# A hybrid GLA / short-convolution layer in fp32r on one core: w_up by 256-column matmuls, nine raw buffers, and attention steps moved

## The chip, the cores and the metric

The kernel runs on one core of a Trainium2 chip. The metric is the device time of one execution in microseconds (us). Three executions of the kernel before took 1450.29, 1451.01 and 1453.19 us; the median is 1451.01 us. One further execution was profiled; it took 1448.84 us, and the profile's span, from the first to the last instruction, is 1447.1 us of that.

## The reference

One layer (DEPTH = 1) over 256 frames of 2048 channels, all in float32:

```python
mod = silu(c) @ w_ada + b_ada                     # 6 vectors of 2048: sh1 sc1 g1 sh2 sc2 g2
h = rmsnorm(x, g0) * (1 + sc1) + sh1
q,k,v,r,lr,cb,cc,cx,ga,gb = split(h @ w_in)       # 512 512 1024 1024 16 1024 1024 1024 2048 2048
log_a = log_sigmoid(lr @ w_a2 + b_a2) / 16
o = gla(q * 128**-.5, k, v, log_a)                # 4 heads, chunks of 64 frames, gated state
y_a = (rmsnorm(o, gla_norm_g) * silu(r)) @ w_out_gla
y_b = (cb * conv3(cc * cx)) @ w_out_conv
x = x + g1 * rmsnorm((sigmoid(ga)*y_a + sigmoid(gb)*y_b) @ w_o, g1n)
h = rmsnorm(x, g2n) * (1 + sc2) + sh2
gate, up = split(h @ w_up)                        # 2 x 5632
x = x + g2 * rmsnorm((gelu(conv3(gate)) * up) @ w_down, g3n)
```

`conv3` is a causal depthwise convolution over three frames. `gla` reads, for each frame of a chunk of 64, the state after that chunk.

## The kernel before

**Arithmetic.** Every large product is made of three TensorE products in the type fp32r. Weights and activations are each split into a high part and a rest: hi is the value cast to fp32r, lo is the value minus hi. A product is hi*hi + hi*lo + lo*hi, accumulated in PSUM.

**Weights** come in chunks of 512 KB (256 rows by 512 columns) by one DMA from SyncE's queue (L278) into a rotating buffer named `raw`. ScalarE casts `raw` to `whi` (L283), VectorE subtracts to make `wlo` (L292). Six `raw` buffers and four of each `whi` and `wlo` rotate. A chunk's `raw` buffer comes free when `wlo` has been made.

**Two forms of product.** `Feat` (L346) keeps the weights as the stationary operand and streams the activations, so its output has channels on partitions and frames in columns. `Tok` (L401) keeps the activations stationary and streams 512 weight columns. `Feat` makes 512 output channels as four blocks of 128 (index j). The activations stand in one tile `H`, for each block of 128 channels 576 columns wide: the first 256 are lo, the next 256 are hi, and behind them, for the feed-forward part, two columns for a shift. For most groups the four blocks share one PSUM tile `mm` of two banks, 256 columns each (`pair=True`). Three `mm` tiles rotate. Two single banks `sm` serve all small products.

**w_up** (`ffn`, 11 pairs of groups, gate and up) is different. The first pair (g = 0) runs on activations that are not yet normalised, by products of 258 columns. For the other 20 groups `both` is set: each block has a whole bank, one matmul of `whi` streams the 512 columns lo and hi of `H` together, and one of `wlo` streams the 256 columns hi into the second half. The two halves of the bank are summed afterwards in `added`: ScalarE copies the first half out (L974), VectorE adds the second (L975). So each chunk (2 blocks of rows, 4 of channels) takes 8 matmuls of 512 and 8 of 256 columns. Then the gate is convolved (`conv`, L616 and L618) and goes through gelu, and the up part is multiplied with it.

**Order.** The whole kernel is a list `stream` of chunks: w_ada's first two vectors together with w_in, then w_in's rest, w_out_conv, w_in's ga, w_out_gla, w_o, and the feed-forward part. Between the chunks stand rows of w_ada for the later vectors (`Gemv`, L439: VectorE multiplies one 512 KB raw buffer with one column of silu(c) and adds it to an accumulator). `pump` walks the list: it issues DMAs up to 10 chunks ahead (`LOOK_DMA`) but never more than the number of raw buffers ahead of the splitting, splits four chunks ahead, and issues the matmuls. A scheduler then sets each engine's order by its own estimate; each engine runs its list strictly in order.

**The attention in the background.** After every chunk of matmuls, `pump` takes one step of a generator `bg`. Beside w_out_conv (24 chunks with w_in's last group ahead of it) that is `gla_gates`: sigmoid of gb, the forget gate, the decayed keys. Beside ga (32 chunks) it is `gla_then_gates`: first `silus` (L670, L671: SiLU of r, four steps), then `gla_heads` with eight steps for each of four heads, then the four sigmoids of ga. That is 36 steps ahead of the sigmoids for 32 chunks; what is left is issued at once (`run_all`). A head is: k^T v (L758), state (L763), q^T S (L772), squares (L776), their sum (L779), a product with ones (L782), square root (L785), reciprocal (L786), scaling (L790, L792), split (L634, L635). The split results are w_out_gla's moving operand, so w_out_gla's last quarter of rows needs the fourth head. `to_rows("g1")` (L819 to L827) sends the vector g1 to memory and back as a row on all partitions.

**Into the feed-forward part.** w_o's last group runs one half of the frames after the other; each half's squares (L833), square root (L850, written r), reciprocal and the new x (L1138) follow, and transposes of x on TensorE (L1152).

Of the kernel before, what the change touches and what calls it, by code (L numbers as in the profile page):

```python
# [15 lines left out]
P = 128  # L16
T = 256
# [20 lines left out]
RAW_BUFS, SPLIT_BUFS, LOOK_SPLIT, LOOK_DMA = 6, 4, 4, 10  # L38
# [23 lines left out]
def hybrid_layer(ctx, tc, x, c, w_ada, b_ada, norm_g, w_in, w_a2, b_a2, gla_norm_g,  # L62
# [127 lines left out]
    def moving():  # L190

        t = sb([P, KD * H_ROW + 32], "H", 1, F32R)[:, 0:KD * H_ROW].rearrange("p (k n) -> p k n", k=KD)
        return t[:, :, T:], t[:, :, 0:T], t[:, :, 0:2 * T]

    h_hi, h_lo, _ = moving()
# [104 lines left out]
    class Feat:  # L300
# [5 lines left out]
        def __init__(self, w, n0, kts, hi, lo, post, row0=0, pair=True, cols=T, per=4, acc=None, both=None):  # L306
            self.both = both
# [17 lines left out]
        def mm(self, ch):  # L325
# [4 lines left out]
            def products(j, passes):  # L330
# [5 lines left out]
                for t in range(ch.n):  # L336
                    for i in passes:
                        w, m = ((ch.hi, self.hi), (ch.hi, self.lo), (ch.lo, self.hi))[i]
                        cols = T if i == 1 else self.cols
                        if self.both and i == 1:  # L340
                            continue
                        if self.both:
                            out, x = (dst[:, T:], m(ch.k0 + t, T)) if i else (dst, self.both(ch.k0 + t))
                        else:
                            out, x = dst[:, 0:cols], m(ch.k0 + t, cols)
                        nc.tensor.matmul(  # L346
                            out, w[:, t, j * P:(j + 1) * P], x,
                            start=first_in_bank and t == 0 and i == 0, stop=end and t == ch.n - 1 and i == 2,
                            skip_group_check=True)
# [335 lines left out]
    def gla_gates():  # L685
# [12 lines left out]
        ps = sm_bank()  # L698
        for k in range(KD):
# [46 lines left out]
    def gla_heads():  # L746
        yield from silus(sr["t"][:, 0])
# [53 lines left out]
    def post_ya(g):  # L801
        def post(j, v):
            if not m_t:
                m_t["hi"], m_t["lo"], _ = moving()
# [162 lines left out]
    xb = lambda k: xs["both"][:, k, :]  # L967
# [4 lines left out]
    def added(dst, ps):  # L972

        nc.scalar.copy(dst, ps[:, :, 0:T])  # L974
        nc.vector.tensor_add(dst, ps[:, :, T:], dst)  # L975
# [9 lines left out]
    def post_gate(g):  # L985
        def post(j, ps):
            if j == 0:
                gl[g] = sb([P, 4, T], "c4", 2)
            pt = padded()
            if g >= N_RAW:  # L990
                added(pt[:, :, 2:], ps)
            else:
                t, b = normed(ps)
                for a in range(2):
                    nc.scalar.activation(pt[:, a, 2:], t[:, a, :], AF.Identity, bias=b[:, a:a + 1])
            cv = tiles(t2())
            conv(cv, pt, lambda i, a: fw(i, 4 * g + j + a))
# [119 lines left out]
    bg = to_rows("g1", gg1, "g8", G8, og["last"])  # L1117
    pump(6, each=step_bg)
# [11 lines left out]
    with tc.high_priority():  # L1130
        xs["hi"], xs["lo"], xs["both"] = moving()
# [90 lines left out]
```

## Time and profile before

| what | value |
|---|---|
| three executions | 1450.29, 1451.01, 1453.19 us |
| the profiled execution | 1448.84 us, its span 1447.1 us |
| granted TensorE clock, mean | 0.993 |
| TensorE busy | 1407.4 us, 97% of the span |
| VectorE, ScalarE busy | 1058.6 us (73%), 816.9 us (56%) |
| read from memory | 363.18 MB, 252 GB/s over the span |
| w_in and w_ada, w_out_conv, w_out_gla, w_o | up to about 695 us |
| feed-forward part | from about 695 us to the end |

Matmuls overlap, and their ends are modelled: a matmul of 256 columns has a mean duration of 278 ns in the groups but starts much closer to the one before. So TensorE's busy share tells little of the pace; that is read from counts over a stretch of time. In a row of the waits the first name waits for the second, with total us, times, and the longest. In a timeline the bracket at the end gives the engine's idle time before the row and what ended it.

### The profile page before, as it was taken

The numbers are of one execution on the slowest core, as the hardware profiler recorded it, in microseconds if no ns is written. First come the engines' busy times: TensorE is split into PE (matmuls) and PEld (weight loads), VectorE is DVE, ScalarE is ACT, GpSimd is POOL, SyncE is SP. The second block draws the span as 40 slices with busy tenths as digits, with TensorE's granted clock in tenths as the row PEclk, the third lists the DMA queues.
The fourth block names the chain that finished last, engine by engine and source line by source line (L and its number), as shares of the span: only waits on it lengthen the run. The fifth ranks groups of instructions, "written<-read, shape, count | busy, mean of one in ns | idle before, by whom it ended". The sixth has DMA issues, their size and how long they took to land.

```text
span 1447.1 us, 23205 instructions
## 1 busy us (share of the span) xinstructions
PE 1407.4 (97%) x9107; PEld 1262.5 (87%) x9107; DVE 1058.6 (73%) x1194; ACT 816.9 (56%) x995; POOL 6.1 (0%) x40
## 2 busy tenths in 40 slices
PE   6999999999999998999999999999999999999997
PEld 6898999898999998988898888888888888888886
DVE  6878888888888777976798777556767645566565
ACT  5789776688574554444665554444545533445553
POOL 0000000000000000000000000000000000000000
PEclk9999999999999999999999999999999999999999
DMA  9999999998979777897467777777786656666652
GB/s 318 329 329 329 373 317 334 335 307 293 355 249 327 244 257 269 293 313 246 134 201 243 227 243 231 248 236 233 230 251 202 217 195 190 186 196 190 190 185 95
DMA packets 177896, 366.82 MB, mean 253 GB/s; under 512 B 13803, under 2 KB 26457, under 8 KB 177018
## 3 DMA queue, kind: packets, MB, share of 16 engines
q1 hardware_dynamic: 176857, 362.17, 76.0%
q0 software_dynamic: 352, 2.11, 0.4%
q8 instruction: 71, 1.16, 0.3%
q10 hardware_dynamic: 576, 1.05, 0.2%
q14 instruction: 40, 0.32, 0.1%
HBM read 363.18 MB, written 2.11 MB: 252 GB/s over the span
## 4 chain that ended last, share of the span: by engine, by line
PE 76%; DMA 11%; DVE 7%; ACT 3%; issue 2%; SPq 0%; DVEq 0%; ACTq 0%
PE mm L346 50%; PE mm L401 25%; DMA raw<-in_w_ada_dram 7%; DMA raw<-in_w_in_dram 4%; DVE wlo L292 2%; ACT whi L283 1%; DVE c L439 1%; DVE c L479 1%; DVE fold L211 0%; PE sm L1152 0%; ACT mm L323 0%; DVE raw L209 0%; PE sm L782 0%; ACT t L257 0%; DVE XF L1138 0%
## 5 line engine op out<-in xcount | busy, mean ns | idle before, releaser
L283 ACT CAST whi<-raw 128x1024 fp32r<-128x1024 f32 (+1 forms) x503 | 513.1, 1025 | 499.1 <-PE mm L346 202.9
L292 DVE TENSOR_TENSOR wlo<-raw,whi 128x1024 fp32r<-128x1024 f32 (+1 forms) x503 | 594.7, 1190 | 245.9 <-ACT whi L283 242.0
L346 PE MATMUL mm<-H,whi 128*128 128x256 f32 (+2 forms) x3712 | 656.9, 321 | 2.2 <-ACT H L254 1.2
L346 PEld LDWEIGHTS mm<-H,whi 128*128 128x128 f32 x3712 | 527.8, 189 | 51.5 <-ACT whi L283 1.7
L346 PE MATMUL mm<-H,wlo 128*128 128x256 f32 (+1 forms) x2496 | 365.9, 278 | 1.4 <-DVE wlo L292 1.4
L346 PEld LDWEIGHTS mm<-H,wlo 128*128 128x128 f32 x2496 | 332.6, 188 | 14.4 <-DVE wlo L292 1.6
L401 PE MATMUL mm<-whi,g 128*128 128x512 f32 x704 | 178.3, 391 | 0.0
L401 PEld LDWEIGHTS mm<-whi,g 128*128 128x128 f32 x704 | 131.9, 188 | 29.1
L439 DVE SCALAR_TENSOR_TENSOR c<-raw,sil,c 128x1024 f32<-128x1024 f32 x90 | 115.3, 1281 | 42.3 <-DMA raw<-in_w_ada_dram 42.1
L401 PE MATMUL mm<-whi,H 128*128 128x512 f32 x448 | 117.5, 394 | 4.2 <-ACT whi L283 4.2
L401 PEld LDWEIGHTS mm<-whi,H 128*128 128x128 f32 x448 | 82.9, 188 | 24.0 <-ACT whi L283 6.4
L401 PE MATMUL mm<-wlo,g 128*128 128x512 f32 x352 | 98.1, 392 | 0.0
L479 DVE SCALAR_TENSOR_TENSOR c<-raw,sil,c 128x768 f32<-128x768 f32 (+2 forms) x73 | 78.6, 1077 | 8.8 <-DMA raw<-in_w_ada_dram 8.1
L401 PEld LDWEIGHTS mm<-wlo,g 128*128 128x128 f32 x352 | 66.1, 188 | 14.1
L401 PE MATMUL mm<-wlo,H 128*128 128x512 f32 x224 | 65.3, 393 | 0.0
L439 DVE SCALAR_TENSOR_TENSOR cb<-raw,sil,cb 128x1024 f32<-128x1024 f32 x30 | 38.5, 1284 | 24.8 <-DMA raw<-in_w_ada_dram 24.8
L401 PEld LDWEIGHTS mm<-wlo,H 128*128 128x128 f32 x224 | 42.2, 188 | 9.0
L618 DVE SCALAR_TENSOR_TENSOR t<-pt,fcol,t 128x256 f32<-128x256 f32 x88 | 36.6, 481 | 0.0
L346 PE MATMUL mm<-B,whi 128*128 128x256 f32 x256 | 33.4, 283 | 0.0
L346 PEld LDWEIGHTS mm<-B,whi 128*128 128x128 f32 x256 | 30.8, 188 | 2.6 <-issue 1.2
L346 PE MATMUL mm<-g,whi 128*128 128x256 f32 x256 | 32.3, 279 | 0.0
L346 PEld LDWEIGHTS mm<-g,whi 128*128 128x128 f32 x256 | 30.8, 190 | 0.0
(196 smaller groups left out, 740.8 us busy)
## 6 DMA issues: line engine op xcount, KB each, us to landing
raw<-in_w_up_dram SPq DMA_DIRECT2D x176, 512.0 KB, 4.3
raw<-in_w_ada_dram SPq DMA_DIRECT2D x160, 512.0 KB, 5.5
raw<-in_w_in_dram SPq DMA_DIRECT2D x145, 512.0 KB, 5.5
raw<-in_w_down_dram SPq DMA_DIRECT2D x88, 512.0 KB, 4.3
raw<-in_w_o_dram SPq DMA_DIRECT2D x32, 512.0 KB, 5.5
raw<-in_w_ada_dram SPq DMA_DIRECT2D x32, 384.0 KB, 5.6
raw<-in_w_out_conv_dram SPq DMA_DIRECT2D x16, 512.0 KB, 5.3
raw<-in_w_out_gla_dram SPq DMA_DIRECT2D x16, 512.0 KB, 5.0
```

Of the source, the lines that this page charges most:

```text
L283: nc.scalar.copy(self.hi, self.raw)
L292: nc.vector.tensor_sub(self.lo, self.raw, f(self.hi))
L346: nc.tensor.matmul(out, w[:, t, j * P:(j + 1) * P], x, start=first_in_bank and t == 0 and i == 0, stop=end and t == ch.n - 1 and i == 2, s ...
L401: nc.tensor.matmul(self.out[s], m(c.k0 + t, T)[:, s * P:(s + 1) * P], w[:, t, :], start=first and t == 0 and i == 0, stop=end and t == c.n ...
L439: nc.vector.scalar_tensor_tensor(a, self.raw, sil[:, self.k:self.k + 1], a, op0=ALU.mult, op1=ALU.add)
L479: nc.vector.scalar_tensor_tensor(a, raw, sc, a, op0=ALU.mult, op1=ALU.add)
L618: nc.vector.scalar_tensor_tensor(dst[:, a, :], pt[:, a, i:T + i], w(i, a), dst[:, a, :], op0=ALU.mult, op1=ALU.add)
```

## The change

Four edits.

- `w_up`: the 20 groups that had `both` now use `pair=True`: three matmuls of 256 columns (`whi` with hi, `whi` with lo, `wlo` with hi) into the same 256 columns of PSUM, four blocks to one `mm` tile. Nothing is left to add: `added` is gone. `post_up` multiplies straight from PSUM. `conv_of` convolves the gate straight from PSUM, with the first two frames handled by shorter operands, so that the padded copy `pt` is not made for these groups. In the last chunk of a group all four blocks end together and `post` is called for two blocks at a time.
- `RAW_BUFS` goes from 6 to 9 and `LOOK_DMA` from 10 to 13. The 12 KB per partition that this takes come from `dynamic_dma_scratch_size`, now 4096 bytes.
- The four `silus` steps stand in `gla_gates`, beside w_out_conv, ahead of the small product with the low-rank gate. `gla_heads` starts with the first head.
- The sigmoids of ga stand in a new generator with `to_rows("g1")`, beside w_out_gla; ga's `done` test is gone.

```diff
-RAW_BUFS, SPLIT_BUFS, LOOK_SPLIT, LOOK_DMA = 6, 4, 4, 10
+RAW_BUFS, SPLIT_BUFS, LOOK_SPLIT, LOOK_DMA = 9, 4, 4, 13
...
-                        if self.both and i == 1:
-                            continue
-                        if self.both:
-                            out, x = (dst[:, T:], m(ch.k0 + t, T)) if i else (dst, self.both(ch.k0 + t))
-                        else:
-                            out, x = dst[:, 0:cols], m(ch.k0 + t, cols)
                         nc.tensor.matmul(
-                            out, w[:, t, j * P:(j + 1) * P], x,
+                            dst[:, 0:cols], w[:, t, j * P:(j + 1) * P], m(ch.k0 + t, cols),
...
         ps = sm_bank()
+        yield from silus(sr["t"][:, 0])
         for k in range(KD):
...
     def gla_heads():
-        yield from silus(sr["t"][:, 0])
...
-    def added(dst, ps):
-
-        nc.scalar.copy(dst, ps[:, :, 0:T])
-        nc.vector.tensor_add(dst, ps[:, :, T:], dst)
+    def conv_of(dst, v, w):
+
+        for a in range(2):
+            nc.scalar.mul(dst[:, a, :], v[:, a, :], w(2, a))
+            for i in (1, 2):
+                nc.vector.scalar_tensor_tensor(dst[:, a, i:], v[:, a, 0:T - i], w(2 - i, a), dst[:, a, i:],
+                                               op0=ALU.mult, op1=ALU.add)
...
-                added(t, ps)
-                nc.vector.tensor_mul(t, t, gl[g][:, j:j + 2, :])
+                nc.vector.tensor_mul(t, ps, gl[g][:, j:j + 2, :])
...
-                ffn += Feat(w_up[0], c0, KD, xh, xl, post, pair=False, cols=T + 2,
-                            both=xb if g >= N_RAW else None).chunks()
+                raw = g < N_RAW
+                ffn += Feat(w_up[0], c0, KD, xh, xl, post, pair=not raw, cols=T + 2 if raw else T, per=2).chunks()
...
-    def gla_then_gates():
-        yield from gla_heads()
-        yield from sigmoids(ga_t["t"], lambda g: ga_t["done"] > g)
-
-    bg = gla_then_gates()
+    bg = gla_heads()
     pump(stream.index(gla_to) + 1 - pos[2], each=step_bg)
     run_all(bg)
...
-    bg = to_rows("g1", gg1, "g8", G8, og["last"])
-    pump(6, each=step_bg)
+
+    def gates_then_row():
+        yield from sigmoids(ga_t["t"])
+        yield from to_rows("g1", gg1, "g8", G8, og["last"])
+
+    bg = gates_then_row()
+    pump(10, each=step_bg)
...
-    nc = _bacc.Bacc("TRN2", target_bir_lowering=False, num_devices=1)
+    nc = _bacc.Bacc("TRN2", target_bir_lowering=False, num_devices=1, dynamic_dma_scratch_size=4096)
```

In the changed kernel the lines behind the first edits have smaller numbers: L346 is L339, L772 is L765, L779 is L772, L782 is L775, L833 is L826, L850 is L843.

**Place 1: TensorE in a w_up group behind the first pair.** `mm` is PSUM, `H` the activations, `whi` and `wlo` the split weights of a chunk. Before:

```order
L346 MATMUL mm_8611<-H_7713,whi_8563 128x512 x4
L346 MATMUL mm_8612<-H_7713,whi_8563 128x512 x4
L346 MATMUL mm_8611<-H_7713,wlo_8565 128x256 x4
L346 MATMUL mm_8612<-H_7713,wlo_8565 128x256 x4
L346 MATMUL mm_8611<-H_7713,whi_8585 128x512 x4
```

After:

```order
L339 MATMUL mm_8313<-H_7719,whi_8239 128x256 x16
L339 MATMUL mm_8313<-H_7719,wlo_8241 128x256 x8
L339 MATMUL mm_8313<-H_7719,whi_8269 128x256 x16
L339 MATMUL mm_8313<-H_7719,wlo_8271 128x256 x8
L339 MATMUL mm_8313<-H_7719,whi_8309 128x256 x16
```

A chunk went from 8 + 8 matmuls on two `mm` tiles to 16 + 8 on one.

**Place 2: TensorE at the fourth head, where ga ends and w_out_gla begins.** `sm_6453` and `sm_6331` are the head's q^T S, `t_991` and `t_982` its sums of squares, `mm_6135` and `mm_6159` the last group of ga, `mm_6427` and `mm_6451` the first group of w_out_gla (its operand `g` is the heads' result). Before:

```order
L346 MATMUL mm_6135<-H_172,wlo_6355 128x256 x8
L772 MATMUL sm_6453<-g_110_527,c_974_6344 128x64 x8
L346 MATMUL mm_6427<-g_850_5453,whi_6390 128x256
L346 MATMUL mm_6427<-g_851_5454,whi_6390 128x256
...
L346 MATMUL mm_6427<-g_850_5453,wlo_6392 128x256
L782 MATMUL sm_6466<-t_991_6464,ones_68 128x256
L346 MATMUL mm_6427<-g_850_5453,wlo_6392 128x256 x7
```

After:

```order
L765 MATMUL sm_6331<-g_113_533,c_963_6224 128x64 x8
L339 MATMUL mm_6159<-H_172,whi_6267 128x256 x16
L339 MATMUL mm_6159<-H_172,wlo_6269 128x256 x8
L339 MATMUL mm_6159<-H_172,whi_6300 128x256 x16
L339 MATMUL mm_6159<-H_172,wlo_6302 128x256 x8
L775 MATMUL sm_6407<-t_982_6372,ones_68 128x256
L339 MATMUL mm_6159<-H_172,whi_6344 128x256 x16
L339 MATMUL mm_6159<-H_172,wlo_6346 128x256 x8
L339 MATMUL mm_6159<-H_172,whi_6376 128x256 x16
L339 MATMUL mm_6159<-H_172,wlo_6378 128x256 x8
L339 MATMUL mm_6451<-g_841_5336,whi_6411 128x256
```

The head's product with ones stood 17 matmuls behind its q^T S, inside w_out_gla's first chunk; it now stands 48 matmuls (two chunks) behind it and two chunks ahead of w_out_gla.

**Place 3: ScalarE at the end of w_o.** The rows are the squares of the second last half, its square root r, and a weight cast. Before:

```order
L283 CAST whi_7638<-raw_7550 128x1024
L833 ACTIVATE t_1198_7682,ys_179<-mm_7531 128x512
L850 ACTIVATE r_38_180<-r_38_180,eps_70 128x1
L283 CAST whi_7656<-raw_7556 128x1024
L833 ACTIVATE t_1199_7706,ys_179<-mm_7532 128x512
L850 ACTIVATE r_38_180<-r_38_180,eps_70 128x1
```

After:

```order
L283 CAST whi_7644<-raw_7507 128x1024
L826 ACTIVATE t_1201_7688,ys_179<-mm_7537 128x512
L843 ACT_TABLE_LOAD
L843 ACTIVATE r_38_180<-r_38_180,eps_70 128x1
L283 CAST whi_7662<-raw_7513 128x1024
L826 ACTIVATE t_1202_7712,ys_179<-mm_7538 128x512
```

ScalarE's last function before this place was a square root (the fourth head's); it is now a sigmoid of ga, and a load of the square root's table stands between the squares and r.

More of the change, by code (lines that the diff above doesn't have):

```diff
@@ L300, in hybrid_layer, with __init__ @@
     class Feat:
-        def __init__(self, w, n0, kts, hi, lo, post, row0=0, pair=True, cols=T, per=4, acc=None, both=None):
-            self.both = both
+        def __init__(self, w, n0, kts, hi, lo, post, row0=0, pair=True, cols=T, per=4, acc=None):
             self.w, self.n0, self.kts, self.hi, self.lo = w, n0, kts, hi, lo
@@ L803, in post @@
             if not m_t:
[L804 removed]
+                m_t["hi"], m_t["lo"] = moving()
             k = 4 * g + j
@@ L988, in post @@
                 gl[g] = sb([P, 4, T], "c4", 2)
-            pt = padded()
+            cv = tiles(t2())
+            w = lambda i, a: fw(i, 4 * g + j + a)
             if g >= N_RAW:
-                added(pt[:, :, 2:], ps)
+                conv_of(cv, ps, w)
             else:
+                pt = padded()
                 t, b = normed(ps)
```

10 lines of the change are left out of this document (4 added, 6 removed).

## The prediction

> **What bounds the kernel now.** I began with the page's busy times and the chain of waits by engine.
>
> ```profile
> PE 1407.4 (97%) x9107; PEld 1262.5 (87%) x9107; DVE 1058.6 (73%) x1194; ACT 816.9 (56%) x995; POOL 6.1 (0%) x40
> PE 76%; DMA 11%; DVE 7%; ACT 3%; issue 2%; SPq 0%; DVEq 0%; ACTq 0%
> ```
>
> TensorE sets the end for most of the span. Where it does, only its pace counts; where DMA, VectorE and ScalarE are on the chain, one must ask whether TensorE stood still. The busy time by stretches tells the two apart (columns: span, then busy us and instruction count of TensorE, its weight loads, VectorE, ScalarE, GpSimd, then clock, DMA share, GB/s):
>
> ```profile
> 150.00:170.00 20.00, 20.00 (x179) 20.00 (x178) 17.07 (x16) 15.17 (x16) 0.00 (x0) 1.00 1.04 385
> 375.00:450.00 75.00, 75.00 (x653) 71.51 (x652) 66.78 (x70) 44.80 (x50) 0.00 (x0) 1.00 0.87 302
> 450.00:575.00 125.00, 117.50 (x981) 114.17 (x980) 96.49 (x104) 62.89 (x69) 1.18 (x2) 0.97 0.80 263
> 780.00:860.00 80.00, 80.00 (x463) 69.69 (x462) 57.60 (x63) 39.00 (x47) 0.31 (x3) 1.00 0.75 238
> ```
>
> From top to bottom: w_in by 256-column matmuls, w_out_conv with the forget gate, ga with the heads, and w_up with 512 and 256 columns mixed. In w_up nothing but TensorE is near its limit. In 450 to 575 us TensorE is idle 7.5 us while the DMA engines are busy only 0.80 of the time. The waits of TensorE between 100 and 600 us name the places:
>
> ```profile
> PE sm L782 <- DVE t L779: 6.3, 2, 5.9
> PE mm L401 <- ACT whi L283: 2.2, 3, 1.0
> PE sm L1093 <- DVE gg L872: 1.9, 1, 1.9
> PE mm L346 <- DVE wlo L292: 1.4, 1, 1.4
> PE sm L782 <- DVE s L870: 1.2, 1, 1.2
> ```
>
> Together 13.0 us; this is all that the edits outside w_up can win.
>
> **The change part by part.**
>
> *w_up.* The groups by shape give the count, the chain in order of time gives the pace (start, us, what, count):
>
> ```profile
> L346 PE MATMUL mm<-H,whi 128*128 128x512 f32 x1280 | 340.2, 395 | 0.0
> 129.30 55.51 PE mm L346 x488
> 1152.03 87.90 PE mm L401 x384
> 1239.93 133.44 PE mm L346 x768
> ```
>
> The last row is w_up: 384 pairs (one of 512, one of 256 columns) in 133.44 us, 347.5 ns a pair. The first of the chain is w_in with three matmuls of 256 in the pair's place: 55.51/488 = 113.7 ns, so 341.2 ns for three. The stretch 150 to 170 us, less the two or three matmuls that overlap its edges, gives 20.00/176.5 = 113.3 and 340.0 ns. The gain is 6.3 to 7.5 ns for each of 1280 pairs, 8.1 to 9.6 us. I take **-8.6 us**. That pace holds with weight loads busy all of the time (20.00 of 20.00 against 69.69 of 80.00 in w_up), which the changed w_up will show too; the same tile `H` and the same `pair` layout in PSUM ran at it. What goes from the other engines lies beside TensorE's work:
>
> ```profile
> L974 ACT COPY t<-mm 128x512 f32<-128x512 f32 x20 | 11.6, 582 | 12.6 <-PE mm L346 12.6
> L975 DVE TENSOR_TENSOR t<-mm,t 128x512 f32<-128x512 f32 x20 | 13.8, 688 | 6.2 <-ACT t L974 6.2
> ```
>
> These and their twins for the gate are 40 x 582 ns and 40 x 688 ns, 23 and 28 us, worth nothing where VectorE has 57.60 of 80.00 us to do. The convolution holds PSUM for longer now. For two blocks it is two operations on ScalarE and four on VectorE, which today read the padded copy:
>
> ```profile
> L616 ACT ACTIVATE t<-pt,fcol 128x256 f32<-128x256 f32 x44 | 19.9, 500 | 0.3
> L618 DVE SCALAR_TENSOR_TENSOR t<-pt,fcol,t 128x256 f32<-128x256 f32 x88 | 36.6, 481 | 0.0
> ```
>
> About 3 us for two blocks and 6 for a group, where a group takes 16 x 4 x 0.34 = 21.8 us and three `mm` tiles rotate, one a group; no tile is awaited. Without that cover it would be up to 6 us for each of ten gate groups.
>
> The Trainium skill's page "TensorE: Matmul & The Clock Gate" (section "Wait — 56ns, not 53.3ns?") gives every warm matmul a fixed cost of about 2.5 ns beside its columns; 1280 more matmuls would cost 3.2 us where I take 8.6 us off. The trace disagrees: two matmuls of 256 at 113.7 ns take 227.4 ns, and one of 512 in w_down (87.90/384) takes 228.9. It is a rival below.
>
> *SiLU and the heads.* The wait of 5.9 us is the fourth head's. TensorE's row, then VectorE's two:
>
> ```profile
> 562.58 1.22 PE L782 MATMUL sm<-t,ones 128*128 128x256 f32 x2 [5.88 <-DVE t L779]
> 560.91 1.28 DVE L439 SCALAR_TENSOR_TENSOR c<-raw,sil,c 128x1024 f32<-128x1024 f32 x1 [3.65 <-DMA raw<-in_w_ada_dram]
> 562.11 0.42 DVE L779 TENSOR_TENSOR t<-t 128x256 f32<-128x256 f32 x1
> ```
>
> L782 is in TensorE's queue 17 matmuls (1.9 us) behind the product that it depends on, and the sum that it needs stands on VectorE behind a row of w_ada whose transfer is late. The change puts two chunks, 48 x 113.7 ns = 5.5 us, between. The first three heads have that distance today and wait 0.4, 1.2 and 0 us (6.3 - 5.9, the row for L870, none). I take 0.6 us left: **-5.3 us**. What is late next? The rest of the head:
>
> ```profile
> 563.84 0.48 ACT L785 ACTIVATE t<-sm,eps 128x256 f32<-128x256 f32 x1 [4.88 <-PE sm L782]
> 571.87 0.69 DVE L635 TENSOR_TENSOR g<-t,g 128x512 fp32r<-128x512 f32 x1 [0.76 <-ACT g L634]
> ```
>
> From 562.58 to the split's end at 572.56 that is 10.0 us. Its reader is w_out_gla's fourth chunk, now five chunks (120 x 113.7 ns = 13.6 us) behind L775, so it is covered with 3.6 us to spare. The sigmoids of ga and the row g1 come up to four chunks, 10.9 us, later; the row is first read 16 chunks (43.7 us) and a group of w_o (96 x 228.9 ns = 22.0 us) after w_out_gla begins, and the first sigmoid is issued three chunks ahead of its reader.
>
> The price is in the stretch that takes the SiLU over:
>
> ```profile
> L671 DVE TENSOR_TENSOR XF<-XF,t 128x512 f32<-128x512 f32 x4 | 2.6, 683 | 0.0
> ```
>
> 2.7 us more for a VectorE that is busy 66.78 of 75.00 us there. All of it fits into the 8.2 us of idle time (0), or all of it reaches TensorE through the forget gate's small products, which stand in TensorE's queue in order (2.7). Most of the idle time is spread in pieces behind ScalarE and transfers, so I take **+1.0 us**.
>
> *Nine raw buffers.* SyncE's queue waits above all for VectorE to free a raw buffer; a transfer then lands 5.5 us after its issue, and ScalarE waits for it:
>
> ```profile
> SPq L278 <- DVE wlo L292: 582.4, 333, 11.4
> raw<-in_w_in_dram SPq DMA_DIRECT2D x145, 512.0 KB, 5.5
> ACT whi L283 <- DMA raw<-in_w_in_dram: 60.4, 50, 4.3
> 353.71 1.22 DVE L292 TENSOR_TENSOR wlo<-raw,whi 128x1024 fp32r<-128x1024 f32 x1 [1.68 <-ACT whi L283]
> 354.86 0.16 DVE L872 TENSOR_TENSOR gg<-sm,bcol 128x8 f32<-128x8 f32 x1
> 506.57 1.28 DVE L439 SCALAR_TENSOR_TENSOR c<-raw,sil,c 128x1024 f32<-128x1024 f32 x1 [1.40 <-DMA raw<-in_w_ada_dram]
> ```
>
> Three more buffers let three more transfers be under way. Where the share is already 1.04 (150 to 170 us) that wins nothing; where it is 0.80 to 0.87, transfers come earlier. Of TensorE's waits, 2.2 us (L401), 1.9 us (L1093, behind the two rows at 353.71) and 1.2 us (L870, behind the row at 506.57) go back to a transfer: 5.3 us. The 1.4 us for `wlo` at 338 us do not. Bounds: 0 to 7.1 us (all waits but the fourth head's). I take three quarters of 5.3: **-4.0 us**. SyncE's order of raw transfers is unchanged; x's second load moves two transfers back.
>
> *The table load at the end of w_o.* Price and path:
>
> ```profile
> L785 ACT ACT_TABLE_LOAD x4 | 5.1, 1283 | 0.1
> 691.61 0.20 ACT L833 ACTIVATION_READ_ACCUMULATOR t<-mm 128x1 f32 x1
> 692.03 0.30 ACT L850 ACTIVATE r<-r,eps 128x1 f32<-128x1 f32 x1 [0.22 <-DVE r L847]
> 692.70 0.76 DVE L1138 SCALAR_TENSOR_TENSOR XF<-A,r,XF 128x512 f32<-128x512 f32 x1
> 693.51 0.44 PE L1152 MATMUL sm<-ident,XF 128*128 128x128 f32 x2
> ```
>
> The load can start at 691.81 and ends at 693.09, so r comes 1.06 us later; TensorE's transposes follow x at 693.51 with 0.05 us to spare, in the midst of w_o's matmuls, which wait behind them. **+1.1 us** (0 if the order shifts, 1.3 at most). The load that `silus` needed goes, but beside other work.
>
> **The sum.** -8.6 - 5.3 + 1.0 - 4.0 + 1.1 = -15.8 us. The profiled execution took 1448.84 us, so 1433.0; the median shown is 2.2 us above it, so **1435 us**.
>
> **The rivals.**
>
> *The transfers decide less than I think.* Raw buffers win nothing, the fourth head keeps half its wait because VectorE's order still holds a row of w_ada ahead of its sum: -8.6 - 2.9 + 1.0 + 1.1 = -9.4, 1442 us. For it: 1.4 us of the waits are VectorE's own. Against: every long wait quoted ends on a transfer.
>
> *They decide more.* With more transfers under way all 13.0 us of waits go and the SiLU is absorbed: -8.6 - 13.0 + 1.1 = -20.5, 1430.5 us. For it: the DMA share of 0.80 while TensorE waits.
>
> *A fixed cost of each matmul.* If w_down's pace per column (228.9/512 = 0.447 ns) were the columns' whole price, a pair's 768 columns would be 343.4 ns and the other 4.1 ns the fixed cost of two matmuls; three would take 349.5, and w_up would lose 2.0 x 1280 = 2.6 us: 1435.2 + 8.6 + 2.6 = 1446 us. The measured w_in stands against it. The Trainium skill's page named above states such a cost, at 2.5 ns.
>
> *All four heads wait like the fourth.* The heads now start right behind the forget gate, in whose stretch VectorE is busiest. If each sum stands behind a late row of w_ada, four waits of 5.9 us take the place of 7.5 us: +16.1 in place of -5.3, 1456.6 us, slower. It decides once the four waits exceed 7.5 + 15.8 - 5.3 + 2.9 = 20.9 us together. Against: two chunks between, and more transfers ahead.
>
> *The change doesn't do what it says*, if small transfers or the software queue with its smaller scratch hold something up: about 1450 us.
>
> **How the numbers follow.** Forecast 0.50, less 0.18, more 0.20, fixed cost 0.05, heads 0.04, last 0.03. The forecast's own range, from the bounds of its terms, is 1430 to 1440; with the neighbours 1426 to 1444. A measurement of this kernel tells about 0.2% (2.9 us) from no change. Faster 0.93, same 0.03, slower 0.04.
>
> **What would show it.** In a w_up stretch of 80 us TensorE should have some 708 matmuls (80/113.3 and the edges), weight loads busy throughout; 1.2 us or less ahead of L775; the waits on `whi` and L1093 gone; the DMA share above 0.87 between 375 and 450 us; a table load of 1.28 us ahead of L843 and about 1 us of wait at the transposes. I am wrong if w_up's pace stays at 347 ns for 768 columns, or if new waits stand in w_out_conv's stretch.

## The result and the profile after

The changed kernel takes 1425.86 us (median of four executions, 1424.5 to 1433.1), the kernel before, run beside it, 1452.1 us. The ratio is 0.9836, with a 95% interval of 0.9814 to 0.9858, that is 23.8 us less (20.6 to 27.0). A second series of the same program gave 0.9848 (0.9829 to 0.9867), 22 us. The profiled execution took 1425.1 us, its span is 1423.4 us: 23.7 us less than the span before. The forecast was 15.8 us.

The page of the changed kernel, busy times and the chain of waits by engine:

```profile
PE 1396.2 (98%) x10387; PEld 1311.1 (92%) x10387; DVE 1034.8 (73%) x1154; ACT 795.3 (56%) x954; POOL 4.0 (0%) x20
PE 86%; DVE 6%; DMA 5%; issue 1%; ACT 1%; DVEq 0%; SPq 0%; ACTq 0%
```

TensorE has 86% of the chain where it had 76%, DMA 5% where it had 11%. TensorE waits less; its own work takes little less (1407.4 to 1396.2 us busy, for 1280 matmuls more). The same four stretches as in the prediction, now of the changed kernel:

```profile
150.00:170.00 20.00, 20.00 (x179) 20.00 (x178) 16.42 (x15) 14.97 (x16) 0.00 (x0) 1.00 1.05 389
375.00:450.00 75.00, 75.00 (x650) 71.11 (x649) 64.16 (x68) 37.95 (x43) 0.00 (x0) 1.00 0.85 295
450.00:575.00 125.00, 124.38 (x1061) 121.31 (x1060) 102.00 (x112) 68.25 (x75) 1.18 (x2) 1.00 0.82 272
780.00:860.00 80.00, 80.00 (x708) 80.00 (x708) 54.55 (x59) 38.19 (x45) 0.00 (x0) 1.00 0.76 241
```

In the third row TensorE is busy 124.38 of 125 us where it was 117.50, and its granted clock is 1.00 where it was 0.97. In the fourth the count is 708, as the prediction said, with weight loads busy throughout. In the second the DMA share is 0.85; the prediction expected more than 0.87. The waits of TensorE between 100 and 600 us, all of at least 0.3 us:

```profile
PE mm L339 <- DVE wlo L292: 0.9, 1, 0.9
PE sm L1088 <- DVE gg L865: 0.8, 1, 0.8
PE mm L339 <- DVE g L628: 0.3, 1, 0.3
```

The five rows of before held 13.0 us, these three hold 2.0, and the fourth head's 5.9 us (L782, now L775) is not among them.

Where the time went is seen where the chain in order of time enters the same work (start, length, count). Before, and then after:

```profile
606.91 74.16 PE mm L401 x324
885.29 52.19 PE mm L401 x228
973.59 141.76 PE mm L346 x816
1118.65 33.38 PE mm L346 x192
```

```profile
589.23 74.16 PE mm L394 x324
865.22 52.19 PE mm L394 x228
953.52 138.74 PE mm L339 x1224
1095.48 33.92 PE mm L339 x288
1129.40 89.60 PE mm L394 x384
1219.00 130.58 PE mm L339 x1152
```

In w_o the changed kernel is 606.91 - 589.23 = 17.7 us ahead, at w_down's first part 20.1 us. All that stands ahead of w_o brought 17.7 us where buffers, SiLU and heads were to bring 8.3 (4.0 + 5.3 - 1.0). w_up brought nearly all of the rest: 816 matmuls (408 pairs) in 141.76 us are now 1224 in 138.74, 3.0 us less. Two rows go the other way: 192 matmuls of w_up in 33.38 us became 288 in 33.92, and w_down's second part, which no edit touches, takes 89.60 us where it took 87.90.

### The profile page after: what moved, and what is told of

It is laid out like the page before. It is cut to its first block, busy times and chain, and to the rows that moved or that the text cites. A ratio compares the mean times of both kernels' runs of the same rounds, so it can differ in the third digit from the quotient of the medians.

```text
span 1423.4 us, 25549 instructions
## 1 busy us (share of the span) xinstructions
PE 1396.2 (98%) x10387; PEld 1311.1 (92%) x10387; DVE 1034.8 (73%) x1154; ACT 795.3 (56%) x954; POOL 4.0 (0%) x20
## 4 chain that ended last, share of the span: by engine, by line
PE 86%; DVE 6%; DMA 5%; issue 1%; ACT 1%; DVEq 0%; SPq 0%; ACTq 0%
PE mm L339 57%; PE mm L394 27%; DMA raw<-in_w_ada_dram 4%; DVE wlo L292 2%; DMA raw<-in_w_in_dram 1%; DVE c L432 1%; PE mm L176 1%; ACT whi L283 0%; DVE c L472 0%; DMA XF<-in_x_dram 0%; DVE fold L211 0%; DVE raw L209 0%; PE sm L1148 0%; DVE t L800 0%; DVE t L779 0%
## 5 line engine op out<-in xcount | busy, mean ns | idle before, releaser
L339 PE MATMUL mm<-H,whi 128*128 128x256 f32 (+1 forms) x4992 | 634.0, 279 | 1.9 <-ACT H L254 1.2
L339 PEld LDWEIGHTS mm<-H,whi 128*128 128x128 f32 x4992 | 600.8, 189 | 5.7 <-issue 1.7
L339 PE MATMUL mm<-H,wlo 128*128 128x256 f32 (+1 forms) x2496 | 341.8, 278 | 0.0
L339 PEld LDWEIGHTS mm<-H,wlo 128*128 128x128 f32 x2496 | 311.1, 188 | 0.1
L969 DVE SCALAR_TENSOR_TENSOR t<-mm,fcol,t 128x255 f32<-128x255 f32 x80 | 38.3, 479 | 1.2
L339 PE MATMUL mm<-B,whi 128*128 128x256 f32 x256 | 33.5, 284 | 0.0
L339 PEld LDWEIGHTS mm<-B,whi 128*128 128x128 f32 x256 | 31.1, 189 | 1.8 <-ACT whi L283 1.2
L339 PE MATMUL mm<-g,whi 128*128 128x256 f32 x256 | 32.4, 278 | 0.3 <-DVE g L628 0.3
L339 PEld LDWEIGHTS mm<-g,whi 128*128 128x128 f32 x256 | 30.4, 188 | 0.7 <-DVE g L628 0.5
```

The costliest lines, as they stand in the source:

```text
L339: nc.tensor.matmul(dst[:, 0:cols], w[:, t, j * P:(j + 1) * P], m(ch.k0 + t, cols), start=first_in_bank and t == 0 and i == 0, stop=end and ...
L969: nc.vector.scalar_tensor_tensor(dst[:, a, i:], v[:, a, 0:T - i], w(2 - i, a), dst[:, a, i:], op0=ALU.mult, op1=ALU.add)
```

## The experiments

All ratios are to the kernel before, run on the same chip in the same series; us are (1 - ratio) x 1451.

| kernel | ratio | interval | us |
|---|---|---|---|
| before + w_up | 0.9954 | 0.9939 to 0.9969 | -6.7 |
| before + nine buffers | 0.9942 | 0.9922 to 0.9963 | -8.4 |
| before + moved steps | 1.0020 | 1.0005 to 1.0034 | +2.9 |
| changed, six buffers, default scratch | 0.9985 | 0.9970 to 0.9999 | -2.2 |
| changed, six buffers, small scratch | 0.9976 | 0.9953 to 0.9998 | -3.5 |
| changed, seven buffers | 0.9846 | 0.9826 to 0.9865 | -22.3 |
| changed, steps back | 0.9893 | 0.9871 to 0.9915 | -15.5 |
| changed, sigmoids of ga back | 0.9835 | 0.9813 to 0.9857 | -23.9 |
| changed, again | 0.9848 | 0.9829 to 0.9867 | -22.1 |
| changed + doubled transposition | 0.9839 | 0.9813 to 0.9864 | -23.4 |
| the same + 512 columns as 2 x 256 | 0.9842 | 0.9822 to 0.9861 | -22.9 |
| changed + product with tri + 2 x 256 | 0.9904 | 0.9875 to 0.9933 | -13.9 |

### Each edit alone

**w_up alone.** The edit of w_up as in the change; buffers, SiLU, heads and sigmoids as before.

> The kernel before with the w_up edit alone (256-column matmuls, added gone, gate convolved from PSUM). Theory of the prediction: a pair of 512+256 columns at 347 ns becomes three of 256 at 340 ns, 1280 times: -8.6 us (-8.1 to -9.6), ratio 0.9941, and w_up in the third part at 130.6 us a 384 pairs in place of 133.4. Rival of a fixed cost of each matmul: +2.6 us, ratio 1.002. A third reading, from the changed kernel's trace: matmuls of 256 columns go at one of two paces, 113.3 or 117.8 ns, and keep it until something else stands between; then the gain lies anywhere from -9.0 us (all at 113.3) down to about -6 (649 matmuls of w_up and w_down at the slower pace, as the changed kernel shows).

Measured: -6.7 us (-4.5 to -8.9). The rival of a fixed cost of each matmul, which would have made it slower, falls. The interval holds both other readings; the chain tells them apart. The chain of this kernel in w_up's second part, w_down's second part and w_up's third:

```profile
967.74 138.75 PE mm L339 x1224
1109.71 33.92 PE mm L339 x288
1143.63 89.60 PE mm L394 x384
1233.23 130.58 PE mm L339 x1152
```

These are the durations of the changed kernel to 0.01 us. 138.75/1224 and 130.58/1152 are 113.4 ns a matmul, 33.92/288 is 117.8 ns, 89.60/384 is 233.3 ns (228.9 before). So the small loss in the middle comes with the w_up edit, and the third reading was the right one: some of the matmuls go at a slower pace, and the gain lies between the two.

**Nine buffers alone.**

```diff
-RAW_BUFS, SPLIT_BUFS, LOOK_SPLIT, LOOK_DMA = 6, 4, 4, 10
+RAW_BUFS, SPLIT_BUFS, LOOK_SPLIT, LOOK_DMA = 9, 4, 4, 13
...
+    nc = _bacc.Bacc("TRN2", target_bir_lowering=False, num_devices=1, dynamic_dma_scratch_size=4096)
```

> The kernel before with nine raw buffers, 13 chunks of look-ahead and the smaller scratch, nothing else. Theory of the prediction: only waits that end on a transfer go, -4.0 us (0 to -7.1), ratio 0.9972. Rival, transfers decide more: stalls also go at the start (-2.2 us by 64 us) and between 130 and 370 us, where the changed kernel's trace is about 8 us ahead: -10 us or more, ratio 0.993 or less; if a late row of w_ada was the whole cause of the fourth head's 5.9 us, that wait goes here too and it is -14 to -16.

Measured: -8.4 us (-5.4 to -11.3), twice the term of 4.0. The interval reaches into the bounds of the theory (0 to -7.1) and into "10 or more". The stretch from 100 to 375 us (w_in beside the rows of w_ada), before, and then with nine buffers:

```profile
100.00:375.00 275.00, 268.65 (x2087) 253.53 (x2086) 230.56 (x242) 215.11 (x248) 0.41 (x4) 1.00 0.95 327
```

```profile
100.00:375.00 275.00, 273.84 (x2179) 261.91 (x2179) 237.94 (x252) 217.69 (x252) 0.42 (x4) 1.00 0.96 339
```

The DMA engines were busy 0.95 of the time before and are busy 0.96 now, but they move 339 GB/s for 327, 3.7% more; 3.7% of 275 us is 10 us. This stretch was limited by its transfers as a whole, with a busy share that looked full. The same work, from the first row of 323 matmuls (72.29 us before, 71.27 now) to the last L1093 (355.07 and 343.56 us), takes 10.5 us less. TensorE's listed waits from 100 to 375 us fell from 6.2 to 1.0 us, which is half of that. The other half stands in no list, and some of it is not the buffers': in the kernel before, 180 matmuls from 287.75 us take 21.21 us, the slower of two paces that are described below. This trace is also of the fastest of six executions (1437.35 us, the median is 1443.51), so it shows more than the -8.4.

The fourth head's wait stays. VectorE's and TensorE's rows of this kernel:

```profile
548.20 0.75 DVE L436 TENSOR_SCALAR c<-raw,sil 128x1024 f32<-128x1024 f32 x1 [3.12 <-DMA raw<-in_w_ada_dram]
548.87 0.42 DVE L779 TENSOR_TENSOR t<-t 128x256 f32<-128x256 f32 x1
549.34 1.22 PE L782 MATMUL sm<-t,ones 128*128 128x256 f32 x2 [5.31 <-DVE t L779]
```

Even with nine buffers a row of w_ada is late and the sum stands behind it. More buffers do not remove this wait.

**The moved steps alone.**

```diff
         ps = sm_bank()
+        yield from silus(sr["t"][:, 0])
...
     def gla_heads():
-        yield from silus(sr["t"][:, 0])
...
-    bg = gla_then_gates()
+    bg = gla_heads()
...
-    bg = to_rows("g1", gg1, "g8", G8, og["last"])
-    pump(6, each=step_bg)
+    bg = gates_then_row()
+    pump(10, each=step_bg)
```

> The kernel before with the moved steps alone: SiLU of r beside w_out_conv, the heads first, the sigmoids of ga beside w_out_gla. Theory of the prediction: -5.3 (the fourth head's wait) +1.0 (VectorE in the gates' stretch) +1.1 (table load) = -3.2 us, ratio 0.9978. Rival, all four heads wait like the fourth: +17 us. Rival, the wait goes and neither price is paid: -5 us or a little more.

Measured: +2.9 us (0.7 to 4.9): slower, against the theory and the third reading, and far from the +17 of the second. The fourth head's product waits no longer, but earlier heads do. TensorE's four largest waits between 64 and 700 us in this kernel:

```profile
PE mm L346 <- DVE wlo L292: 3.1, 3, 2.0
PE sm L758 <- DVE t L790: 2.4, 1, 2.4
PE sm L782 <- DVE t L779: 2.4, 1, 2.4
PE mm L401 <- DVE wlo L292: 2.3, 2, 1.4
```

The two rows for heads (2.4 us each) lie at 472 and 484 us, with 0.9 us at L772 and 0.4 us at L758 beside them: 6.1 us in place of the 7.5 of before. Ahead of the sum that the first of them waits for, VectorE has a late row of w_ada:

```profile
469.44 1.29 DVE L439 SCALAR_TENSOR_TENSOR c<-raw,sil,c 128x1024 f32<-128x1024 f32 x1 [3.40 <-DMA raw<-in_w_ada_dram]
```

Further on, between 586 and 622 us, TensorE waits 3.4 us for `wlo` of w_out_gla and w_o; the kernel before has no such wait there. (2.0 of the 3.1 us in the first row lie at 340 us, ahead of the moved steps.) What ScalarE's cast of the weights waited for between 560 and 640 us (w_out_gla and the start of w_o), before, and then with the moved steps:

```profile
ACT whi L283 <- DMA raw<-in_w_out_gla_dram: 9.8, 5, 3.2
ACT whi L283 <- DMA raw<-in_w_o_dram: 6.5, 5, 2.6
```

```profile
ACT whi L283 <- DMA raw<-in_w_out_gla_dram: 13.1, 5, 5.6
ACT whi L283 <- DMA raw<-in_w_o_dram: 12.1, 6, 4.3
```

16.3 us became 25.2. So with six buffers the steps win little at the heads, and TensorE then waits for the weights of w_out_gla and w_o.

### Which resource the steps need

**Six buffers in the changed kernel**, first with the default scratch:

```diff
-RAW_BUFS, SPLIT_BUFS, LOOK_SPLIT, LOOK_DMA = 9, 4, 4, 13
+RAW_BUFS, SPLIT_BUFS, LOOK_SPLIT, LOOK_DMA = 6, 4, 4, 10
...
-    nc = _bacc.Bacc("TRN2", target_bir_lowering=False, num_devices=1, dynamic_dma_scratch_size=4096)
+    nc = _bacc.Bacc("TRN2", target_bir_lowering=False, num_devices=1)
```

> The changed kernel with six raw buffers, 10 chunks of look-ahead and the default scratch again. Theory of the prediction: 4 us above the changed kernel, about 12 us below the kernel before when w_up gives 8.6 and the steps 3.2. Rival, transfers decide more: 8 to 12 us above the changed kernel, ratio to the kernel before 0.990 to 0.993.

Measured: -2.2 us, so 20 us above the changed kernel, and outside both expectations. w_up's -6.7 and the steps' +2.9 add up to -3.8, which the interval (-4.4 to -0.1) holds. The same with the scratch left at 4096 bytes, so with the first two lines of that diff alone:

> The changed kernel with six raw buffers and 10 chunks of look-ahead, the scratch left at 4096 bytes. Its instructions and their order are those of the run with six buffers and the default scratch (-2.2 us to the kernel before); only the scratch differs. Seven buffers gave -22.4 us, nine -23.8. Theory that the buffers decide: the seventh buffer carries nearly all, and this kernel stands at -2 us (ratio 0.997 to 1.000), with the waits for wlo near 600 us and the fourth part of the span above. Rival that the scratch decides: the small scratch is what moves the transfers, the buffers bring little, and this kernel stands at -20 us or lower (0.984 to 0.988).

Measured: -3.5 us (-0.3 to -6.8). The scratch is not the cause. **Seven buffers**, small scratch (in all these runs the look-ahead goes with the buffers; no run tells the two apart):

```diff
-RAW_BUFS, SPLIT_BUFS, LOOK_SPLIT, LOOK_DMA = 9, 4, 4, 13
+RAW_BUFS, SPLIT_BUFS, LOOK_SPLIT, LOOK_DMA = 7, 4, 4, 11
```

> The changed kernel with seven raw buffers and 11 chunks of look-ahead in place of nine and 13, scratch left small. With six it stood at -2.2 us to the kernel before, with nine at -23.8. If each buffer adds its share, seven gives -9 us (ratio 0.994). If the first one or two already bridge the late transfers, -17 us or more (0.988 or less). If the scratch and not the buffers were the cause, it equals the changed kernel (0.984).

Measured: -22.3 us. One buffer more than six carries all that nine carry, within the intervals. ScalarE's waits between 560 and 640 us, with six (small scratch) and then with seven buffers, where the second row is no longer in the list:

```profile
ACT whi L283 <- DMA raw<-in_w_out_gla_dram: 19.3, 7, 6.1
ACT whi L283 <- DMA raw<-in_w_o_dram: 8.2, 4, 3.6
```

```profile
ACT whi L283 <- DMA raw<-in_w_out_gla_dram: 4.2, 3, 2.9
```

27.5 us of waits for these transfers became 4.2, and TensorE's own waits for `wlo` in the same stretch, 4.8 us with six, are gone with seven. The trace with six buffers is of the slowest of twelve executions (1459.8 us, the median is 1445.9), so it shows more than the 19 us between the two ratios.

### What the steps are worth beside nine buffers

**The changed kernel again**, unaltered.

> The changed kernel once more, unaltered, for its time beside the three below and for a second trace. All theories: ratio 0.984 (-23.8 us). What it tells: whether the stretches in which matmuls of 256 columns start every 117.8 ns in place of 113.3 (in the first trace 348 to 425 us and 1095 to 1219 us, 572 and 649 matmuls) stand at the same places. If the order of the instructions sets them, they do, and the span agrees within 1 us; if timing of the single execution does, some are gone or new, and the time moves by 4.4 ns for each matmul.

Measured: -22.1 us. The two long stretches of 117.8 ns that the expectation names are there again; others are new (below), and the span is 4 us longer. So both readings hold in part.

**Steps back**: the diff of the moved steps, undone in the changed kernel.

> The changed kernel without the moved steps: w_up edit and nine buffers, SiLU of r ahead of the heads, sigmoids of ga behind them. If the three edits add up (-6.7 for w_up, -8.4 for the buffers, +2.9 for the steps, together -12.2), this kernel is at -15.1, and the changed kernel, at -23.8, has 8.7 us that no edit alone shows. Theory now: the moved steps need the nine buffers. They are worth +2.9 us with six and -8.7 us with nine, so this kernel stands at -15 us, ratio 0.9896, with the fourth head's wait of about 5.3 us still there. Rival: the nine buffers need w_up's edit (less work for VectorE and ScalarE), then it stands at -20 or lower.

Measured: -15.5 us (-12.3 to -18.7). That is the sum of w_up (-6.7) and the buffers (-8.4), so these two add up; the rival that the buffers need the w_up edit falls. The steps are worth 6.5 to 8.3 us beside nine buffers (0.9848 and 0.9836 against 0.9893, a difference that is uncertain by some 4 us), and with six they cost 2.9 us in the kernel before and 3.2 to 4.5 us beside the w_up edit. TensorE's wait at the product with ones in this kernel is back:

```profile
PE sm L775 <- DVE t L772: 3.4, 1, 3.4
```

**Sigmoids of ga back**, the SiLU left beside w_out_conv:

```diff
-    bg = gla_heads()
+    def gla_then_gates():
+        yield from gla_heads()
+        yield from sigmoids(ga_t["t"], lambda g: ga_t["done"] > g)
+
+    bg = gla_then_gates()
...
-    bg = gates_then_row()
-    pump(10, each=step_bg)
+    bg = to_rows("g1", gg1, "g8", G8, og["last"])
+    pump(6, each=step_bg)
```

> The changed kernel with the sigmoids of ga behind the heads again, the SiLU of r left beside w_out_conv. If the two chunks between sum and product are what removes the fourth head's wait, this stays: within 2 us of the changed kernel (ratio 0.983 to 0.986), with no wait above 1.2 us at the product with ones, and no table load in w_o's end. If the sigmoids were the other half of the gain, it loses 3 to 5 us.

Measured: -23.9 us, and no wait at the product with ones in the list of TensorE's waits. What removes the wait is the SiLU's move, which gives the heads their distance; where the sigmoids of ga stand makes no difference that can be measured. The table load at w_o's end, which was not to be there, is there. Here too the last sigmoid of ga now comes behind the fourth head's square root: ScalarE loads the square root's table at 540.76 us (L778) and the sigmoid's at 547.61 us (L656). In the kernel before the square root came last (L663 at 555.30, L785 at 557.67 us). So it is the heads' earlier end that brings the load, not the move of the sigmoids.

**Where each edit acts.** Two small products of TensorE stand in every trace: the last L1093 (now L1088), at the end of w_in beside the rows of w_ada and ahead of the moved steps, and L151, behind w_o and ahead of the groups of w_up that the change touches. In the kernel before:

```profile
355.07 0.28 PE L1093 MATMUL sm<-ident,t 66*128 66x66 f32 x1 [1.88 <-DVE gg L872]
719.73 0.68 PE L151 MATMUL sm<-t,ones 128*128 128x128 f32 x4 [0.20 <-DVE t L150]
```

The spans, cut at these two, in us:

| kernel of the trace | start to L1093 | L1093 to L151 | L151 to the end |
|---|---|---|---|
| before | 355.1 | 364.7 | 727.4 |
| before + w_up | 353.9 | 362.4 | 721.0 |
| before + nine buffers | 343.6 | 364.4 | 727.3 |
| before + moved steps | 355.5 | 368.8 | 728.3 |
| changed, steps back | 344.8 | 363.1 | 722.2 |
| changed | 343.6 | 358.4 | 721.4 |
| changed, again | 347.5 | 358.7 | 721.2 |

The nine buffers win ahead of L1093 and, without the moved steps, next to nothing behind it. The w_up edit wins behind L151. The moved steps act between the two: they lose 4.1 us there with six buffers and win 4.4 to 4.7 us with nine. For the changed kernel that is 11.5, 6.3 and 6.0 us, which is the whole difference of the spans. These are single executions; the two of the changed kernel are 4 us apart, all of it ahead of L1093.

### The pace of the matmuls

The 672 matmuls (288 + 384) at the slower pace cost 672 x 4.44 ns = 3.0 us in every kernel with the w_up edit whose products with 512 columns are whole. They begin where the row g2 is transposed, in the changed kernel here:

```profile
1095.21 0.27 PE L812 MATMUL sm<-ident,gg 128*16 128x128 f32 x1
```

Three kernels try to turn the pace back or to use it.

**A doubled transposition**:

```diff
+        if name == "g2":
+            yield
+            nc.tensor.transpose(ps[0:KD, 0:P], cols, ident)
```

> The changed kernel with one matmul more: the transposition that starts the row g2 is issued twice, one chunk of w_up apart, into the same place. In eight of eight places of the traces so far that transposition turned the pace of the matmuls over, 113.3 to 117.8 ns or back, and in every kernel with the w_up edit it left 672 matmuls of w_up and w_down (about 1095 to 1219 us) at the slower pace, 3.0 us. Theory that the pace is a state that such a small matmul turns over: the slow stretch is 24 matmuls long in place of 672 and the kernel gains 2.8 us, ratio about 0.982. Rival that the pace follows from the work of that stretch (transfers, tiles): the stretch stays slow and the time stays at 0.984.

Measured: 0.9839, no gain, and the chain shows why (from the second transposition on):

```profile
1106.65 31.10 PE mm L339 x264
```

31.10/264 is still 117.8 ns. The theory that such a matmul always turns the pace over falls; in the kernel with six buffers and the small scratch, too, the transposition of the row g1 leaves the faster pace as it was. **512 columns as 2 x 256**, on top of it:

```diff
-                        nc.tensor.matmul(
-                            self.out[s], m(c.k0 + t, T)[:, s * P:(s + 1) * P], w[:, t, :],
-                            start=first and t == 0 and i == 0,
-                            stop=end and t == c.n - 1 and i == 2, skip_group_check=True)
+                        for h in range(2):
+                            n = slice(h * T, (h + 1) * T)
+                            nc.tensor.matmul(
+                                self.out[s][:, n], m(c.k0 + t, T)[:, s * P:(s + 1) * P], w[:, t, n],
+                                start=first and t == 0 and i == 0 and h == 0,
+                                stop=end and t == c.n - 1 and i == 2, skip_group_check=True)
```

> As the run with the doubled transposition, and the products with 512 weight columns (w_down, w_o and others, 1728 matmuls) as two of 256 columns each with the same stationary operand. By the faster paces 2 x 113.3 ns take the place of 228.9, 2.2 ns for each of 1728, -3.8 us, ratio about 0.980. If a slow pace, which the step from 256 to 512 columns ended in eight of eight places, now runs on into w_down, it loses 4.4 ns on each of up to 1152 matmuls, +5 us, and the sum is near or above the run without it. If a cost of each matmul decides (the rival of the prediction), it is slower by 1728 x 2.5 ns = 4.3 us or more.

Measured: 0.9842, the same. The rows for w_down's first and second part:

```profile
866.88 51.68 PE mm L396 x456
1131.67 90.45 PE mm L396 x768
```

At the faster pace 456 halves take 51.68 us where 228 whole ones took 52.19 (2.2 ns less for each, as expected); at the slower pace 768 halves take 90.45 us where 384 took 89.60 (2.2 ns more). The one cancels the other, because the slow stretch stays. Nor does the step to 512 columns end a slow stretch, as the expectation has it: the 384 products of the changed kernel go slowly in 89.60 us, and the faster pace is back with the 256 columns behind them (130.58 us for 1152). **A product with tri in place of the second transposition**, its result unread:

```diff
-        nc.tensor.transpose(ps[0:KD, 0:P], cols, ident)
+        turn = nc.tensor.transpose(ps[0:KD, 0:P], cols, ident)
+        if name == "g2":
+            with tc.issue_after(turn.ins):
+                nc.tensor.matmul(sm_bank(), tri, xin["t"][:, 0, 0:512], start=True, stop=True)
```

> The changed kernel with two additions. The products with 512 weight columns go as two of 256, as in the run before it; and behind the transposition that starts the row g2 stands one product with the triangular matrix tri over 512 columns of x, whose result nobody reads, in place of the doubled transposition. Doubling did not bring the faster pace back: 1031 matmuls behind it (1097 to 1222 us) started every 117.8 ns. The product with tri stands, in the traces so far, 12 times ahead of the pace of 113.3 ns and never ahead of 117.8. Theory that the interrupting matmul's form sets the pace: behind it the spacing is 113.3 ns to the end of w_down, 1031 x 4.4 ns = 4.6 us won for 0.9 us that the product takes, -3.7 us to the run with the doubled transposition (1427.4 us), ratio about 0.981. Rival that the stretch itself (its tiles and transfers) sets it: 117.8 ns stays and it costs 0.9 us, ratio 0.985.

```profile
1097.43 33.92 PE mm L339 x288
1131.36 90.45 PE mm L396 x768
```

The pace stays at 117.8 ns behind it too, so at this place the form of the matmul that interrupts does not set it. Its time, 0.9904, is 9 us above the run before it, far more than the 0.9 us of the product; its profiled execution took 1427.1 us, less than the median of 1435.5, and does not show where the others (up to 1448.3 us) lost it. What sets the pace and what these executions lost stay open. None of these variants beats the changed kernel measurably.

## Why the prediction was right, and where it was not

The direction and the mechanisms of w_up and of the fourth head's wait were right. The size was 8 us short: 1425.86 us lies below the forecast's own range (1430 to 1440 us) and just at the edge of the wider one (1426). The likeliest rival, "they decide more" at 1430.5 us, came nearer and was still too cautious. The order of the terms came out otherwise: the forecast put w_up first and the buffers last, and alone the buffers brought 8.4 us, w_up 6.7. That w_up fell 1.9 us short while two prices, 2.1 us together, were not paid cancels by luck, so the 8 us are about what the buffers and the steps won beyond their terms.

*w_up, -8.6.* Measured alone: -6.7 (-4.5 to -8.9, which holds the term). The gain of a pair is as worked out: 3.0 us for 408 pairs and 133.44 - 130.58 = 2.9 us for 384 are 7.4 ns each, between the 6.3 and 7.5 of the prediction. What the term lacked is the slower pace in the second part: 33.92 for 33.38 us, and 89.60 for 87.90, 2.2 us given back, most of it at a place that the edit does not touch. The Trainium skill's fixed cost ("TensorE: Matmul & The Clock Gate", section "Wait — 56ns, not 53.3ns?") would have made w_up slower and the halved w_down too. The traces disagree at the faster pace (51.68 against 52.19 us); at the slower one a fixed part of that size is seen (90.45 against 89.60 us).

*Nine buffers, -4.0, bounds 0 to -7.1.* This is the mis-sized term: -8.4 alone and, beside the w_up edit, -8.8 (0.9893 against 0.9954). Its interval still reaches into the bounds. Two steps were the mistake. "This is all that the edits outside w_up can win" took the list of waits (13.0 us in 100 to 600 us) for the whole price, and about half of what the trace with nine buffers wins up to L1093 is not in that list. "Where the share is already 1.04 (150 to 170 us) that wins nothing" is right for these 20 us (385 and 389 GB/s, as many matmuls); carried over to the whole stretch from 100 to 375 us it is not, where the share was 0.95, and yet 327 GB/s became 339. The gain at the start, 1.0 us by 72 us, was not in the bounds either.

*SiLU and the heads, -5.3.* The cause was right: the fourth head's wait goes by distance, not by earlier transfers (5.3 us remained with nine buffers alone; none at that place after). Two things were left out. First, what stands around the wait has to be ready. With six buffers it is not: rows of w_ada are late at other heads and `wlo` of w_out_gla and w_o is late behind them, and the steps alone lose 2.9 us. The prediction asked "what is late next" only of the fourth head's own chain. Second, this wait costs more than its length. In the kernel before the granted clock is 0.50 from 559 to 563 us, within the fourth head's wait, and 0.56 on the mean in the 3 us behind it (the columns are those of the stretches above):

```profile
563.00:566.00 3.00, 3.00 (x15) 2.82 (x15) 2.51 (x2) 1.41 (x2) 0.00 (x0) 0.56 0.58 182
```

At 113.4 ns 3 us hold 26 matmuls, and here are 15. The 20 matmuls of w_out_gla's first two chunks from 563.24 to 566.87 us take 3.6 us where they should take 2.3, so some 1.4 us come on top of the 5.9. The prediction's third row had shown the clock of 0.97; it is 1.00 now. Beside nine buffers the steps are worth 6.5 to 8.3 us by the times, whose uncertainty also holds 5.3, and 4.4 to 4.7 us by the traces. In the kernel with the steps back there are 3.4 us of wait at the head and 2.0 us behind a row of w_ada.

*VectorE, +1.0.* Not seen: in 375 to 450 us TensorE is busy 75.00 of 75.00 us with no wait in the list, and 650 matmuls stand for 653. Delays too small for the list would not show here.

*Table load, +1.1.* The load came, the cost did not. ScalarE's and TensorE's rows of the changed kernel:

```profile
674.13 1.28 ACT L843 ACT_TABLE_LOAD   x1
676.89 0.27 PE L1148 MATMUL sm<-ident,XF 128*128 128x128 f32 x1
680.16 0.87 PE L1148 MATMUL sm<-ident,XF 128*128 128x128 f32 x6 [2.42 <-DVE XF L1134]
```

The first transposition has no wait ahead of it: in the new order it stands later among w_o's matmuls. The wait of 2.42 us at the second half was there before with 2.4, and from w_o's first matmul to L151 it is 112.9 us where it was 113.0. The prediction named this case ("0 if the order shifts") and took the other.

*The rivals.* "All four heads wait" is not seen with nine buffers; a milder form of it (6.1 us in all) is in the kernel with the steps alone, which is slower, as that rival would have it, but by 2.9 us.

## What to carry to other kernels

A wait that is removed is worth only as much as what stands next is ready: the same move cost 2.9 us with six buffers and won 6.5 to 8.3 us with nine, so edits that feed each other have to be timed together as well as alone. Where transfers set the pace of a stretch, read its GB/s and its matmul count beside the list of waits and the busy share, which went from 0.95 to 0.96 while 3.7% were won. Read the granted clock behind a wait as well as the wait's length. One buffer more, with its look-ahead, was enough here; seven did what nine do.

## What the runs showed of the hardware

Matmuls of one shape go at one of two paces, and keep it over hundreds of matmuls. 256 columns start every 113.4 or every 117.8 ns, 512 columns every 228.9 or every 233.3 ns: 4.4 ns for each matmul, whatever its columns. The granted clock is 1.00 in both. The changed kernel, at the slower pace, and 291 matmuls in 34 us:

```profile
1095.00:1129.00 34.00, 34.00 (x291) 33.99 (x290) 18.40 (x21) 15.13 (x19) 1.05 (x2) 1.00 0.67 217
```

The same work in w_up's first part, in the changed kernel (whose row for w_down, 52.19 us for 228, stands above), and then in the one with the sigmoids of ga back, which does not differ from it there, with w_down behind it:

```profile
753.77 111.45 PE mm L339 x981
```

```profile
755.07 115.81 PE mm L339 x981
870.88 53.20 PE mm L394 x228
```

4.4 us for 981 matmuls and 1.0 us for 228. Two executions of the changed kernel differ like this as well, early in w_in (54.16 and 56.26 us for 476 matmuls):

```profile
128.44 54.16 PE mm L339 x476
```

```profile
129.90 56.26 PE mm L339 x476
```

So the order of the instructions alone does not set it, though one stretch (g2's transposition to the end of w_down's second part) had the slower pace in every kernel with 256 columns in w_up. In the traces the pace changes where something else stands between, such as a small product, a wait or a change of shape. What sets it stays open. It moves single executions by several us, about as much as a small edit of this kernel is worth, so a single trace is weak evidence for such an edit.
